# A hybrid encoder block: sums and low halves on GpSimd around each change of part of the down projection, its first pair reordered, and late query splits

## The chip, the cores and the metric

The kernel runs on one core of one Trainium2 chip. The metric is the device time of one execution in microseconds (us); what is compared are medians over several executions. A core has five engines that each work through their own queue in order: TensorE (PE, matrix products; its weight loads are listed apart as PEld), VectorE (DVE), ScalarE (ACT), GpSimd (POOL) and SyncE (SP), which here issues the transfers (DMA) between the device's memory and the on-chip buffer SBUF. PE writes its results to a second, small buffer, PSUM. Engines wait for each other through semaphores.

## The reference, cut to what matters

```python
h = x                                                     # 2048 x 1024, float32
xn = rms_norm(h, ln_mix_g)
proj = xn @ w_in
y_a = mlstm_group(...)                                    # 4 heads x 128, both directions
y_b = mla_group(...)                                      # 4 heads, softmax over 2048 keys
h = h + concatenate([y_a, y_b]) @ w_out
# conv_gated_mlp, D_FF = 2816
u = dwconv3_centred(rms_norm(h, ln_ffn_g) @ w_up, conv_w, conv_b)
gate, val = split(u, 2)
h = h + (silu(gate) * val) @ w_down
# per-layer input
gate = sigmoid(rms_norm(h, ple_norm_g) @ w_ple_gate)
h = h + gate * rms_norm(p @ w_ple_proj, ple_post_g)
out = rms_norm(h, final_g)
```

The change touches the attention and mLSTM stage (only when its steps are issued), the projection `w_down`, and the last stage.

## The kernel before, in words

**Precision.** All products are float32 results made of three products: each operand is split into a high half (a rounded copy, by ACT) and a low half (the operand less its high half, by DVE: a subtraction, line 120, in `split`), and `mm3` (line 130) adds low x high, high x low and high x high into PSUM. So one product of two 128-wide blocks is three PE instructions.

**Stages.** `run` issues them in order: the input projection, attention with the mLSTM as a side generator beside it, the output projection, `up_down` (up projection, convolution, down projection), and `ple` (the last stage, whose preparation runs as a generator beside the last pairs of down). All instructions are issued by one Python program; a scheduler then sets the order on each engine, so that the order of the built program can differ from the order of the lines. SBUF is divided into named places (`self.at("t7", ...)`); a second tile at the same place waits until the readers of the first are done. Places and PSUM tiles are what couples the steps.

**Attention** (from line 1000). 64 steps (head, query tile), each with a written order of operations; every "." in it is a place where `pump` may advance the mLSTM generator, `SIDE` of 832 times in all. In the generator, `pause(n)` yields n times between a step's vector work and its products. `load_q` and `split_q` load the queries of a pair of query tiles and split them.

**Up and down** (`up_down`, line 1387 on). Each stage is cut into *pairs* i: pairs 0 to 21 are the first half of the sequence of the up projection (block 0), 22 to 43 the second (block 1), and 44 to 51, 52 to 59 and 60 to 67 are down, whose inner dimension (22 tiles of 128) is cut into three parts of 8, 8 and 6 tiles (blocks 2 to 4); part after part is added to h. Within a pair the 2 x 2 blocks are multiplied with seven products in place of eight (Strassen's scheme in Winograd's form): A11 B11, S1 T1, S2 T2, A12 B21, S3 T3, A22 T4 and S4 B22, each of 12 PE instructions of 128x512 (9 in block 4). The right-hand tiles B and T belong to a block and stay in SBUF for all its pairs; at a *change of part* they are loaded and split anew, by `load_op`, tile by tile, through a few rotating raw buffers ("opr"). The left-hand tiles belong to a pair: `up_load` loads them two pairs ahead (in down: "hraw", the hidden activations that the convolution stored), `up_prep` makes the four sums S1 to S4 of them one pair ahead (four 128x512 additions, lines 1361 to 1369) and splits them by `up_pair` ("fw").

The seven products of a pair go to two PSUM tiles, one with halves x and y ("fxy"), one with halves z and spare ("fzs"). The products A22 T4 and S4 B22 of a pair are issued in the next pair (`rest(prev)`), where they add to y and z. In the up projection, results go to "ug" and "uv", which `conv` takes through the convolution and the gate to `hid_d`. In down they are added to two rows of h ("fh", loaded by `down_out` into five rotating places, o[0] and o[1], stored when the pair is done). p1, a copy of the first product, is made by ACT (line 1493) for i up to 44.

Pair 44 is special: it is down's first, and `conv` of pair 43 runs inside it; the second row of h is loaded to the place "u2", which is uv of pair 43, so its load (line 1325) is issued when that convolution is done. The adds of p1, T3 and z into that row follow the load.

**The last stage** (`ple`, the loop over 16 tiles of 128 rows). For each: the products with `w_ple_proj` ("pjp"), the next tile's p load (line 1580) and transposes ("nt_p", line 1603), the load of h for the tile after (line 1587) with its square sum ("junk", line 1589) and normalisation ("xn", line 1594), 48 products with `w_ple_gate` in two halves of columns, then the final norm: squares (line 1688), reduction (1692), gain (1690 and 1693), scale and two stores (1695 to 1698). h has three places in turn, so the load for tile st + 2 waits until the stores of tile st - 1 have gone out.

Of the kernel before, what the change touches and what calls it, by code (L numbers as in the profile page):

```python
# [19 lines left out]
P = 128  # L20
# [16 lines left out]
LAG_T, LAG_X, LAG_R = 1, 2, 2  # L37
SIDE = 621
KSCALE = 128.0 ** -0.5
# [21 lines left out]
class Block:  # L61
# [679 lines left out]
    def mlstm(self):  # L741
# [17 lines left out]
        def state(r, j, kk, v1, old, new):  # L759
            kn, kw = kk[:, 0], kk[:, 1]  # L760
            nc.vector.scalar_tensor_tensor(kw, kn, KSCALE, hc("w", r, j).unsqueeze(2).broadcast_to([P, NH, P]),
                                           op0=ALU.mult, op1=ALU.mult)
            yield from pause(6 if (r, j) == (1, 0) else 3)
            for hp in range(2):
# [35 lines left out]
        for c in range(NT):  # L800
# [21 lines left out]
            if c == 0:  # L822
                yield from pause(5)
            mk2 = self.at("w9", [P, 2, NH, P], name="mk")
# [135 lines left out]
    def attend(self, side):  # L960
# [60 lines left out]
        for i, (h, qt) in enumerate(seq):  # L1021
# [8 lines left out]
            nxt = start(*seq[i + 1]) if i + 1 < len(seq) else None  # L1030
            if qt % 2 == 0 and i + 2 < len(seq):
                split_q(seq[i + 2][0], seq[i + 2][1] // 2)
            if nxt is None:
                self.ps0 = self.pml.tile([P, 512], F32, name="wo0", tag="ml")
                self.out_mm(self.ps0, self.y0, range(4), slice(0, 512))
            for op in order:
# [6 lines left out]
                elif op == "X" and nxt:  # L1043
                    soft(nxt)
                elif op[0] == "e" and nxt:
                    expo(nxt, int(op[1]))
                elif op[0] == "E" and i:
                    expo(cur, int(op[1]))
                elif op == "V" and qt % 2:
                    pend = Tile()  # L1050
                    pend.h, pend.pr, pend.pts = h, qt // 2, pts
                    pv(pend, 0)
                elif op == "V" and pend is not None:
                    pv(pend, 1)
            if qt % 2:
                pts = []
# [201 lines left out]
    def load_op(self, blk, n):  # L1258

        ops = self.xop[n] = self.op_places(blk, n)  # L1260
        for k, (hi, lo) in enumerate(ops):
# [11 lines left out]
            self.nc.sync.dma_start(raw, src)  # L1273
            self.split(raw, hi, lo)

# [65 lines left out]
    def up_prep(self, i):  # L1341
# [15 lines left out]
        else:  # L1357
            sv, sg = flat(raw[1]), g
            lo, hi = slice(0, n // 2), slice(n // 2, n)
            tt = nc.vector.tensor_tensor  # L1360
            tt(sv[:, hi], sv[:, lo], sv[:, hi], op=ALU.add)
# [14 lines left out]
    def up_down(self, out):  # L1376
# [90 lines left out]
        for i in range(n):  # L1467
# [16 lines left out]
            x, s.y, s.z, s.spare = xy[:, 0], xy[:, 1], zs[:, 0], zs[:, 1]  # L1484
            prod(x, s.ops["A11"], "B11")
            if s.down:
                s.o = outs.pop(i)
                add(s.o[0][:, H], s.o[0][:, H], x)
            if i > NUP:
                add(twice(s.o[1]), twice(s.o[1]), x.unsqueeze(1).broadcast_to([P, 2, SB]))  # L1490
            else:
                s.p1 = self.at(f"t{6 + i % 2}", [P, SB], name="p1")
                nc.scalar.copy(s.p1, x)
            if i == 0:
# [39 lines left out]
            if i == NUP - 1:  # L1534
                outs[NUP] = self.down_out(NUP, (0,))
            if i == NUP:
                s.o += self.down_out(NUP, (1,))
                add(twice(s.o[1]), twice(s.o[1]), s.p1.unsqueeze(1).broadcast_to([P, 2, SB]))
            if s.down and i + 1 < n:
                outs[i + 1] = self.down_out(i + 1)  # L1540
            prod(s.y, s.ops["S3"], "T3", True)
            if s.down:
                add(s.o[1][:, H], s.o[1][:, H], s.y)
# [19 lines left out]
    def ple(self, out):  # L1563
# [99 lines left out]
        for st in range(NT):  # L1663
# [15 lines left out]
            for i in range(len(cuts) - 1):  # L1679
# [8 lines left out]
                nc.scalar.activation(gt[:, fs], h2[:, fs], AF.Square, accum_out=s2[:, i:i + 1])  # L1688
                if cuts[i + 1] < D:
                    nc.vector.tensor_tensor(h2[:, fs], h2[:, fs], gfin[:, fs], op=ALU.mult)  # L1690
            st2 = self.stat(1, "ps3")
            nc.vector.tensor_reduce(st2, s2, axis=AX.X, op=ALU.add)  # L1692
            nc.vector.tensor_tensor(h2[:, fs], h2[:, fs], gfin[:, fs], op=ALU.mult)
            r2 = self.rsq(st2, 1, 1.0 / D)
# [51 lines left out]
```

## Time and profile before

| | |
|---|---|
| median of 3 executions | 2996.68 us (2990.95 to 2999.37) |
| profiled execution, its own time | 2998.91 us |
| its span in the profile | 2997.1 us |
| granted PE clock, mean | 0.994 |
| PE busy / DVE / ACT / POOL | 98% / 69% / 45% / 5% of the span |
| PE busy, 1255 to 1800 us (up projection, first half, and what leads to it) | 542.11 of 545 us |
| PE busy, 1800 to 2300 us (up projection, second half, and the start of down) | 492.03 of 500 us |
| PE busy, 2300 to 2750 us (down) | 429.53 of 450 us |
| PE busy, 2750 to 2997 us (last stage) | 232.94 of 247 us |

How rows of the profile are read. A timeline row has its start and length in us, the engine, the line, the operation, the names (out<-in), shapes, the count of like instructions in a row, and in brackets the idle time before it with what ended it: `[10.88 <-DVE fh L1380]` means that the engine stood 10.88 us and was released by the DVE instruction of line 1380 that wrote fh. A wait row ("engine line waited for") has the total, the number of times and the longest. A group row has busy time and mean ns of one, then the idle time before. A row "SPq" is the issue of a transfer; the transfer itself lands some us later. A window row has start:end and length, then busy time and count for PE, PEld, DVE, ACT and POOL, the granted PE clock, the DMA engines' share and GB/s. A row of one line or operation gives shortest/median/longest duration in ns.

### The profile page before, as it was taken

How to read it: one execution, taken by the hardware profiler on the slowest of the kernel's cores; microseconds unless marked ns; L12 is line 12 of the kernel's file. 1: busy time of each engine (PE TensorE's matmuls, PEld its weight loads, DVE VectorE, ACT ScalarE, POOL GpSimd, SP SyncE). 2: the span in 40 equal slices, each digit the busy share in tenths (PEclk: the TensorE clock that was granted, in tenths of full speed). 3: DMA queues.
4: the chain of work that ended last, by engine and by line, in shares of the span. 5: the costliest groups of instructions: out<-in, count | busy, mean ns of one | idle time of the engine just before them, and what ended most of it. 6: DMA issues, size and time to landing. Idle time of an engine off the chain costs nothing. (4 is left out here: it accounts for less than half of the span.)

```text
span 2997.1 us, 40676 instructions
## 1 busy us (share of the span) xinstructions
PE 2926.3 (98%) x14858; PEld 2457.2 (82%) x14858; DVE 2069.6 (69%) x3798; ACT 1347.3 (45%) x2645; POOL 148.0 (5%) x262
## 2 busy tenths in 40 slices
PE   8999999999999999999999999999998999999998
PEld 7888888888898888888788887788886787877777
DVE  7431556667777677636888888877779778787555
ACT  7211545555666565523544445444445132233444
POOL 3100000000000001001000000000000000000111
PEclk9999999999999999999999999999999999999999
DMA  6522445343333333568664345833336868575221
GB/s 196 107 76 88 137 130 165 109 149 99 102 101 97 94 124 105 177 211 277 221 216 138 136 140 191 263 123 125 127 122 195 266 216 291 185 247 182 73 77 64
DMA packets 377400, 460.19 MB, mean 154 GB/s; under 512 B 30176, under 2 KB 263152, under 8 KB 377200
## 3 DMA queue, kind: packets, MB, share of 16 engines
q1 hardware_dynamic: 377200, 457.59, 47.5%
q8 instruction: 117, 1.92, 0.3%
q14 instruction: 83, 0.68, 0.1%
HBM read 294.26 MB, written 163.25 MB: 153 GB/s over the span
## 5 line engine op out<-in xcount | busy, mean ns | idle before, releaser
L130 PE MATMUL fxy<-op,fw 128*128 128x512 f32 x3168 | 754.1, 395 | 15.9 <-DVE fh L1380 8.4
L130 PEld LDWEIGHTS fxy<-op,fw 128*128 128x128 f32 x3168 | 591.4, 189 | 162.1 <-DVE fh L1380 19.2
L130 PE MATMUL fzs<-op,fw 128*128 128x512 f32 x1584 | 385.8, 389 | 0.8 <-DVE xt L1151 0.8
L130 PEld LDWEIGHTS fzs<-op,fw 128*128 128x128 f32 x1584 | 297.1, 188 | 63.0 <-DVE xt L1151 1.0
L130 PE MATMUL bk<-wsp,xh 128*128 128x512 f32 (+1 forms) x768 | 234.4, 386 | 1.1 <-DVE wsp L126 1.1
L117 ACT CAST pt<-tb 128x512 fp32r<-128x512 f32 x256 | 146.5, 587 | 194.5 <-PE tb L976 193.9
L918 DVE TENSOR_REDUCE mx<-bk 128x1 f32<-128x512 f32 x256 | 174.8, 685 | 46.3 <-PE bk L917 45.4
L130 PE MATMUL fxy<-op,fwd 128*128 128x512 f32 x792 | 193.1, 393 | 12.8 <-DVE fh L1380 10.9
L130 PE MATMUL ppv<-pt,kv 128*128 128x256 f32 x1536 | 203.0, 287 | 0.0
L120 DVE TENSOR_TENSOR pt<-tb,pt 128x512 fp32r<-128x512 f32 x256 | 174.0, 686 | 33.6 <-ACT pt L117 31.9
L130 PEld LDWEIGHTS ppv<-pt,kv 128*128 128x128 f32 x1536 | 188.7, 191 | 0.4 <-ACT pt L117 0.4
L130 PEld LDWEIGHTS fxy<-op,fwd 128*128 128x128 f32 x792 | 149.3, 189 | 46.0 <-DVE fh L1380 12.1
L936 ACT ACTIVATE pe<-bk,nm 128x512 f32<-128x512 f32 x256 | 174.5, 696 | 25.4 <-DVE nm L930 24.5
L130 PE MATMUL pgp<-pw,x3s 128*128 128x512 f32 (+1 forms) x792 | 179.0, 385 | 0.8 <-DVE pw L120 0.8
L130 PE MATMUL bk<-wo,yhl 128*128 128x512 f32 x744 | 175.6, 392 | 0.0
L130 PEld LDWEIGHTS pgp<-pw,x3s 128*128 128x128 f32 x792 | 144.4, 188 | 29.7 <-DVE pw L120 1.1
L130 PEld LDWEIGHTS bk<-wsp,xh 128*128 128x128 f32 x768 | 144.6, 189 | 27.5 <-DVE wsp L126 2.4
L130 PEld LDWEIGHTS bk<-wo,yhl 128*128 128x128 f32 x744 | 138.2, 188 | 28.0
L1380 DVE TENSOR_TENSOR fh<-fh,fxy 128x512 f32<-128x512 f32 x143 | 108.4, 770 | 75.8 <-PE fxy L130 74.6
L130 PE MATMUL bk<-wsp,xl 128*128 128x512 f32 (+1 forms) x384 | 150.7, 392 | 7.4 <-DVE xl L120 7.4
L130 PE MATMUL bk<-xh,wqk 128*128 128x512 f32 x480 | 157.3, 393 | 0.0
L117 ACT CAST fw<-hraw 128x1024 fp32r<-128x1024 f32 (+1 forms) x72 | 70.5, 981 | 187.3 <-PE fxy L130 114.6
(327 smaller groups left out, 5030.0 us busy)
## 6 DMA issues: line engine op xcount, KB each, us to landing
fwr<-in_w_up SPq DMA_DIRECT2D x66, 512.0 KB, 4.2
fh<-h_d SPq DMA_DIRECT2D x48, 512.0 KB, 4.8
h_d<-fh SPq DMA_DIRECT2D x48, 512.0 KB, 2.9
s_d<-fwr SPq DMA_DIRECT2D x44, 512.0 KB, 3.2
fws<-s_d SPq DMA_DIRECT2D x44, 512.0 KB, 3.7
rw<-row_d SPq DMA_DIRECT2D x32, 512.0 KB, 5.2
hraw<-hid_d SPq DMA_DIRECT2D x30, 512.0 KB, 4.8
tsum<-in_w_down SPq DMA_DIRECT2D x44, 256.0 KB, 4.4
```

Of the source, the lines that this page charges most:

```text
L117: nc.scalar.copy(hi, src)
L120: (sub or nc.vector).tensor_tensor(lo, src, _f(hi), op=ALU.subtract)
L130: mm = lambda *a, **k: self.nc.tensor.matmul(*a, **k, skip_group_check=more)
L918: nc.vector.tensor_reduce(s.mx[:, kb:kb + 1], ps, axis=AX.X, op=ALU.max)
L936: nc.scalar.activation(s.pe[:, kb % 2], s.banks[kb], AF.Exp, bias=s.nm, scale=ASCALE, accum_out=s.rs[:, kb:kb + 1])
L1380: add = lambda o, a, b: tt(o, a, b, op=ALU.add)
```

## The change

In words, by the parts of the diff:

- The mLSTM generator is advanced 629 times rather than 621 over the attention, and two of its pauses are four yields longer.
- `split_q` is called behind a step's order of operations instead of ahead of it.
- `load_op`: the low halves of T4 and B22 of the three down blocks are subtracted on GpSimd.
- `up_prep`: for the pairs 44 to 46, 51 to 54 and 59 to 62 the four sums are made on GpSimd.
- `up_down`: pair 45 copies its first product as well (to the spare half of its second PSUM tile, where pairs 0 to 44 use an SBUF place), and the adds of pairs 44 and 45 read the copy. In pair 44 the sum p1 + T3 + z is made in "t7"; only then the second row of h is loaded, and p1 and that sum are added to its two halves. The rows of pair 45 are loaded behind that, not ahead of T3.
- `ple`: for all but the last tile the second half's gain is multiplied ahead of the reduction rather than behind it.

```diff
--- before.py
+++ after.py
@@ -35,7 +35,7 @@
 EPS = 1e-6
 SB = 512
 LAG_T, LAG_X, LAG_R = 1, 2, 2
-SIDE = 621
+SIDE = 629
 KSCALE = 128.0 ** -0.5
 ASCALE = 192.0 ** -0.5
 
@@ -760,7 +760,7 @@
             kn, kw = kk[:, 0], kk[:, 1]
             nc.vector.scalar_tensor_tensor(kw, kn, KSCALE, hc("w", r, j).unsqueeze(2).broadcast_to([P, NH, P]),
                                            op0=ALU.mult, op1=ALU.mult)
-            yield from pause(6 if (r, j) == (1, 0) else 3)
+            yield from pause(10 if (r, j) == (1, 0) else 3)
             for hp in range(2):
                 ps = mbank([P, 2, 256])
                 for i in range(2):
@@ -820,7 +820,7 @@
                 else:
                     nc.sync.dma_start(kk[:, 0], self.kn_d[c])
             if c == 0:
-                yield from pause(5)
+                yield from pause(9)
             mk2 = self.at("w9", [P, 2, NH, P], name="mk")
             qi2 = self.at("w10", [P, 2, NH, P], name="qi")
             for r in range(2):
@@ -1028,8 +1028,6 @@
             if qt % 2 == 1 and i + 3 < len(seq):
                 load_q(seq[i + 3][0], seq[i + 3][1] // 2)
             nxt = start(*seq[i + 1]) if i + 1 < len(seq) else None
-            if qt % 2 == 0 and i + 2 < len(seq):
-                split_q(seq[i + 2][0], seq[i + 2][1] // 2)
             if nxt is None:
                 self.ps0 = self.pml.tile([P, 512], F32, name="wo0", tag="ml")
                 self.out_mm(self.ps0, self.y0, range(4), slice(0, 512))
@@ -1052,6 +1050,8 @@
                     pv(pend, 0)
                 elif op == "V" and pend is not None:
                     pv(pend, 1)
+            if qt % 2 == 0 and i + 2 < len(seq):
+                split_q(seq[i + 2][0], seq[i + 2][1] // 2)
             if qt % 2:
                 pts = []
             cur = nxt
@@ -1257,6 +1257,7 @@
 
     def load_op(self, blk, n):
 
+        nc = self.nc
         ops = self.xop[n] = self.op_places(blk, n)
         for k, (hi, lo) in enumerate(ops):
             raw = self.at(next(self.orot), [P, SB], name="opr")
@@ -1271,7 +1272,7 @@
             else:
                 src = self.w_down(blk - 2, k, 2 * (int(n[1]) - 1) + int(n[2]) - 1)
             self.nc.sync.dma_start(raw, src)
-            self.split(raw, hi, lo)
+            self.split(raw, hi, lo, sub=nc.gpsimd if blk > 1 and n in ("T4", "B22") else None)
 
     def up_load(self, i):
 
@@ -1357,7 +1358,8 @@
         else:
             sv, sg = flat(raw[1]), g
             lo, hi = slice(0, n // 2), slice(n // 2, n)
-            tt = nc.vector.tensor_tensor
+            change = any(-2 < i - bl[0] < 3 for bl in self.BLOCKS[2:])
+            tt = (nc.gpsimd if change else nc.vector).tensor_tensor
             tt(sv[:, hi], sv[:, lo], sv[:, hi], op=ALU.add)
             tt(sv[:, lo], g[:, lo], sv[:, lo], op=ALU.subtract)
         ops["S3"], ops["S1"] = self.up_pair(sv)
@@ -1483,14 +1485,15 @@
             xy, zs = self.two([P, 2, SB], "fxy"), self.two([P, 2, SB], "fzs")
             x, s.y, s.z, s.spare = xy[:, 0], xy[:, 1], zs[:, 0], zs[:, 1]
             prod(x, s.ops["A11"], "B11")
+            if i < NUP + 2:
+                s.p1 = s.spare if i > NUP else self.at(f"t{6 + i % 2}", [P, SB], name="p1")
+                nc.scalar.copy(s.p1, x)
             if s.down:
                 s.o = outs.pop(i)
-                add(s.o[0][:, H], s.o[0][:, H], x)
+                p1 = s.p1 if i < NUP + 2 else x
+                add(s.o[0][:, H], s.o[0][:, H], p1)
             if i > NUP:
-                add(twice(s.o[1]), twice(s.o[1]), x.unsqueeze(1).broadcast_to([P, 2, SB]))
-            else:
-                s.p1 = self.at(f"t{6 + i % 2}", [P, SB], name="p1")
-                nc.scalar.copy(s.p1, x)
+                add(twice(s.o[1]), twice(s.o[1]), p1.unsqueeze(1).broadcast_to([P, 2, SB]))
             if i == 0:
                 load(0, "B21")
             load(then, "B11")
@@ -1533,13 +1536,18 @@
                 conv(prev)
             if i == NUP - 1:
                 outs[NUP] = self.down_out(NUP, (0,))
-            if i == NUP:
-                s.o += self.down_out(NUP, (1,))
-                add(twice(s.o[1]), twice(s.o[1]), s.p1.unsqueeze(1).broadcast_to([P, 2, SB]))
-            if s.down and i + 1 < n:
+            if i > NUP and i + 1 < n:
                 outs[i + 1] = self.down_out(i + 1)
             prod(s.y, s.ops["S3"], "T3", True)
-            if s.down:
+            if i == NUP:
+                c22 = self.at("t7", [P, SB], name="c22")
+                add(c22, s.p1, s.y)
+                add(c22, c22, s.z)
+                s.o += self.down_out(NUP, (1,))
+                add(s.o[1][:, L], s.o[1][:, L], s.p1)
+                add(s.o[1][:, H], s.o[1][:, H], c22)
+                outs[i + 1] = self.down_out(i + 1)
+            elif s.down:
                 add(s.o[1][:, H], s.o[1][:, H], s.y)
                 add(s.o[1][:, H], s.o[1][:, H], s.z)
             else:
@@ -1686,11 +1694,12 @@
                 nc.vector.tensor_tensor(pj[:, fs], pj[:, fs], gt[:, fs], op=ALU.mult)
                 nc.vector.tensor_tensor(h2[:, fs], h2[:, fs], pj[:, fs], op=ALU.add)
                 nc.scalar.activation(gt[:, fs], h2[:, fs], AF.Square, accum_out=s2[:, i:i + 1])
-                if cuts[i + 1] < D:
+                if st < NT - 1 or cuts[i + 1] < D:
                     nc.vector.tensor_tensor(h2[:, fs], h2[:, fs], gfin[:, fs], op=ALU.mult)
             st2 = self.stat(1, "ps3")
             nc.vector.tensor_reduce(st2, s2, axis=AX.X, op=ALU.add)
-            nc.vector.tensor_tensor(h2[:, fs], h2[:, fs], gfin[:, fs], op=ALU.mult)
+            if st == NT - 1:
+                nc.vector.tensor_tensor(h2[:, fs], h2[:, fs], gfin[:, fs], op=ALU.mult)
             r2 = self.rsq(st2, 1, 1.0 / D)
             nc.vector.tensor_scalar(h2[:, 0:512], h2[:, 0:512], r2, None, op0=ALU.mult)
             nc.sync.dma_start(out[0, st * P:(st + 1) * P, 0:512], h2[:, 0:512])
```

## The prediction, made blind

> **What bounds the kernel now.** I read the busy shares first, then what TensorE (PE) waited for, then stretches of 150 us through the down projection, then the order of single instructions where a stretch falls short.
>
> ```profile
> span 2997.1 us, 40676 instructions
> PE 2926.3 (98%) x14858; PEld 2457.2 (82%) x14858; DVE 2069.6 (69%) x3798; ACT 1347.3 (45%) x2645; POOL 148.0 (5%) x262
> ...
> PE fxy L130 <- DVE fh L1380: 19.3, 8, 10.9
> PE nt_p L1603 <- DVE xn L1594: 6.1, 9, 1.0
> PE mb L768 <- DVE kk L761: 2.8, 1, 2.8
> ...
> 2100.00:2250.00 150.00, 150.00 (x662) 123.58 (x661) 108.54 (x127) 67.00 (x87) 0.00 (x0) 1.00 0.39 125
> 2250.00:2400.00 150.00, 130.24 (x542) 104.03 (x541) 120.74 (x166) 52.18 (x73) 0.00 (x0) 0.94 0.72 232
> 2400.00:2550.00 150.00, 147.08 (x636) 119.29 (x635) 116.70 (x161) 44.25 (x58) 0.00 (x0) 0.99 0.74 252
> ```
>
> PE is busy for 2926.3 of 2997.1 us, so only its idle time, 70.8 us, and time at a lowered clock can be won without taking products out, and the change takes none out. In the stretch columns (span, then PE, PEld, DVE, ACT, POOL busy with their counts, granted clock, DMA share, GB/s) the stretch from 2100 shows PE full: 662 products in 150 us, 0.2266 us each. From 2250, where the up projection turns into down, there are 120 fewer: 120 x 0.2266 = 27.2 us lost, of them 150 - 130.24 = 19.8 idle and 7.4 at a clock of 0.94. From 2400 (change to the second part of down) 26 fewer lose 5.9, of them 2.9 idle. Those two places are what the change can mostly reach. The next view shows them, product by product.
>
> ```profile
> 2295.74 3.02 PE L130 MATMUL fxy<-op,fw 128*128 128x512 f32 x12 [2.02 <-ACT p L1493]
> 2299.63 3.02 PE L130 MATMUL fxy<-op,fw 128*128 128x512 f32 x12 [0.88 <-DVE fh L1380]
> 2304.44 7.36 PE L130 MATMUL fxy<-op,fw 128*128 128x512 f32 x24 [1.79 <-DVE fw L120]
> 2311.63 2.88 PE L130 MATMUL fzs<-op,fw 128*128 128x512 f32 x12
> 2325.40 4.68 PE L130 MATMUL fxy<-op,fwd 128*128 128x512 f32 x12 [10.88 <-DVE fh L1380]
> ...
> 2478.88 10.03 PE L130 MATMUL fxy<-op,fw 128*128 128x512 f32 x36 [2.92 <-DVE fh L1380]
> ```
>
> These rows are, by the order of the built program: T2 of pair 44, its B21, then its T3 between two halves of B11 of pair 45, T1 of 45, and T4 of 44, which waits 10.88 us. The 12 products behind the wait take 4.68 instead of 2.88. At 2478.88 stands the same thing, smaller, in pair 52.
>
> Who is late at 2325.40? VectorE (DVE) and the SP queue say it:
>
> ```profile
> 2289.01 3.10 DVE L120 TENSOR_TENSOR op<-opr,op 128x512 fp32r<-128x512 f32 x5
> ...
> 2306.11 1.28 DVE L1423 SCALAR_TENSOR_TENSOR fgv<-ug,fcw,fgv 128x1024 f32<-128x1024 f32 x1
> 2314.86 1.22 DVE L120 TENSOR_TENSOR fw<-hraw,fw 128x1024 fp32r<-128x1024 f32 x1
> 2318.67 0.68 DVE L1380 TENSOR_TENSOR fh<-fh,fxy 128x512 f32<-128x512 f32 x1
> 2322.92 1.23 DVE L1380 TENSOR_TENSOR fh<-fh,p 128x1024 f32<-128x1024 f32 x1 [1.39 <-DMA fh<-h_d]
> 2324.66 0.68 DVE L1380 TENSOR_TENSOR fh<-fh,fxy 128x512 f32<-128x512 f32 x1
> ...
> 2317.30 0.33 SPq L1325 DMA_DIRECT2D fh<-h_d  x1
> ```
>
> Two things in a row. DVE works through a queue (splits, convolution of pair 43, sums of the next pair's tiles) and comes to the add of B21 only at 2318.67, though those products, begun at 2299.63, had ended before 2304.44. Then the load of h, issued at 2317.30 because its buffer holds the last convolution, is waited for until 2322.92, and T3's add comes at 2324.66. T4 writes the PSUM buffer which that add reads.
>
> **The change part by part.**
>
> *First pair of down.* Its correction term c22 = p1 + T3 + z is added up in an SBUF buffer before h is there, so PSUM is free without the load. Leaving the load and its 1.23 us add out alone brings the two adds of T3 and z from 2324.66 to about 2319.3 (right behind 2318.67 + 0.68): -5.4 us. p1 is copied by ScalarE for pairs 44 and 45 at once; the row at 2295.74 shows what such a copy can cost, 2.02 us, and in the new order it stands ahead of the copies of streamed tiles that wait for DMAs, so I take up to that off. What moves behind: the add of h's load for pair 45 now also waits for loads queued later on SP, and T1 of pair 45 waits for it. Product order in the built program: T2(44), B21(44) and T3(44) with B11(45) in three pieces between them, T2(45), T4(44), B22(44), B21(45), T1(45). By T4 there are 60 products in either order, and T1(45) comes 31 products x 0.2266 = 7.0 us behind T4's start at the earliest, where a load (5.6 us from 2317.30 to 2322.92) fits. I cost it at nothing; without that cover it is 1 to 3 us.
>
> *Work taken from DVE.* Low halves of T4 and B22 (8 per change of part, 6 in the last) and four sums for each of 11 pairs (three or four to a change), 66 operations of 128x512 in all, go to GpSimd (POOL). Five splits in a row take 3.10 (0.62 each), so until T4(44) DVE gives up 8 splits and 4 to 8 sums, 7 to 10 us of its 25 us queue. POOL takes them up. Before's trace has no two-input POOL operation of that size:
>
> ```profile
> L140 POOL TENSOR_TENSOR rsr<-rsm,nhalf 128x1 f32<-128x1 f32 (+2 forms) x96 | 67.3, 702 | 8.0
> L830 POOL TENSOR_SCALAR_AFFINE_SELECT mk<-rw 128x512 f32<-128x512 f32 x32 | 25.7, 827 | 912.0 <-PE mb L768 547.5 <-PE mb L853 273.9 <-DVE mx L918 68.6
> ...
> 910.62 1.67 POOL L830 TENSOR_SCALAR_AFFINE_SELECT mk<-rw 128x512 f32<-128x512 f32 x2 [23.59 <-DVE mx L918]
> ...
> 910.88 0.92 DVE L835 TENSOR_TENSOR qi<-qk,rw 128x512 f32<-128x512 f32 x1
> 911.79 1.04 DVE L835 TENSOR_TENSOR qi<-qk,rw 128x512 f32<-128x512 f32 x1
> ...
> L830 POOL TENSOR_SCALAR_AFFINE_SELECT mk<-rw x32: 634/638/1169, 663.0 to 1197.9; 128x512 f32<-128x512 f32 x32
> ...
> L835 DVE TENSOR_TENSOR qi<-qk,rw x32: 665/914/1046, 659.4 to 1199.2; 128x512 f32<-128x512 f32 x32
> ```
>
> Bounds: 0.70 us (a POOL tensor-tensor of one column, nearly all fixed cost) and 1.65 (two selects of 0.827 mean, one per input). I take 1.2, the middle, as nothing puts it nearer to either. [...]
>
> ```profile
> 2301.30 1.21 ACT L117 CAST op<-opr 128x512 fp32r<-128x512 f32 x2 [0.26 <-DMA opr<-in_w_down]
> 2308.02 1.05 ACT L117 CAST fw<-hraw 128x1024 fp32r<-128x1024 f32 x1 [5.51 <-DVE hraw L1362]
> ```
>
> The queue on POOL by the program: T4's four subtractions, three sums of pair 45, then B22's with the last sum. The last streamed raw tile lands at 2301.3, so with some seven operations then still ahead the fourth sum ends near 2301 + 7 x 1.2 = 2309.4; a copy by ScalarE and a split by DVE (1.05 and 1.22) make the S2 weights ready at 2311.7, against 2316.1 before (2314.86 + 1.22). T2(45) waits for them. Behind that split on DVE stand, by the program, what is left of the convolution (two or three operations of 1.28 like the row at 2306.11), the short ones for its edge, and c22, which so comes near 2317, 5 us later. PE: 48 products from T2(44)'s start without the 2.02, at 2293.7, end at 2304.6 plus 1 or 2 us of small waits; it then waits some 5 us for T2(45), and some 3 for c22. T4(44) starts at 2317 rather than 2325.4: -8.4. The lost clock I leave as it is (two shorter waits for one long one); at best 4 us of its 7.4 come back. Range of this part: -13 to +6 (the rival below).
>
> *Second part of down.* The wait of 2.92 stands behind an add of DVE that is queued among eight splits of streamed tiles (0.62 each), each waiting for its load's copy. These go to POOL. The wait and its slow clock (36 products in 10.03 rather than 36 x 0.2266 = 8.2) are worth 2.9 + 1.8 = 4.7; I take -2.9, bounds -4.7 and +3. The third part shows no wait worth naming and is put at 0.
>
> *The last loop (per-layer input).* For 15 tiles the second gain multiply stands ahead of the reduce, and the built program has the next p load ahead of both output stores on SP.
>
> ```profile
> 2861.61 0.33 SPq L1696 DMA_DIRECT2D out<-h  x1
> 2862.04 0.55 SPq L1580 DMA_DIRECT2D p_t<-in_p_turned  x1
> 2862.64 0.60 SPq L1698 DMA_DIRECT2D out<-h  x1
> 2865.39 0.33 SPq L1587 DMA_DIRECT2D h<-h_d  x1
> ...
> 2868.97 1.06 ACT L1589 ACTIVATE junk<-h 128x1024 bf16<-128x1024 f32 x1 [3.62 <-DMA h<-h_d]
> ...
> 2859.64 0.15 DVE L1692 TENSOR_REDUCE ps<-ps 128x1 f32<-128x2 f32 x1 [0.85 <-ACT gate L1688]
> 2859.71 0.68 DVE L1693 TENSOR_TENSOR h<-h,gpf 128x512 f32<-128x512 f32 x1
> ...
> 2871.96 1.23 PE L1603 MATMUL nt_p<-ident,xn 128*128 128x128 f32 x8 [0.67 <-DVE xn L1594]
> ```
>
> The loop's round is a chain: second output store, load of h into the freed buffer, square, normalisation, transposes. Without p's issue (0.55) between the stores the round shortens by up to 0.55, the wait of 0.67 almost wholly. Against that the reduce moves behind the multiply: DVE was idle 0.85 ahead of the reduce, waiting for the square, so the multiply (0.68) may fit there, and if it doesn't, it costs 0.68. Nine waits cost 6.1; I take half, -3. Bounds: -6.1, and +6 (9 x 0.68).
>
> *Pauses and late query splits.* The side generator's count (629 for 621) and two longer pauses move mLSTM work against attention. In the built program the product that waits 2.76 for kk keeps its place in PE's queue, and the query splits still come some two tiles ahead of their use: 0, bounds ±2.8.
>
> Sum: -8.4 - 2.9 - 3 + 0 = -14.3. The profiled execution took 2998.91 us (1.8 around its span), 2.2 above the median of 2996.68, so 2984.6; I don't take the 2.2 off again, as single runs lay from 2990.95 to 2999.37, and say 2984.
>
> **The rivals.**
>
> *DVE and POOL hold each other up.* In the rows at 910 two selects and two DVE multiplies with SBUF inputs took 2.2 us together, where alone they take 2 x 0.634 and 2 x 0.665 (the fastest of each), 2.6 in series: beside each other they hardly run faster than one after the other. If each POOL operation stops DVE for its whole length, 20 of them up to the end of pair 45 cost 20 x (1.2 - 0.62) = 11.6 us of DVE's queue. From T4(44) that takes back the 5.4 of the load and 6 more: +6. In the second part the 20 cost as much, less DVE's idle share there (116.70 of 150 busy, so 22% of some 36 us, 8): +4. With -3 in the last loop: +7, 3006. It decides from a POOL operation of 0.62 + 5.4/20 = 0.9 us on. For it: the slowed multiplies, and a saturated DVE. Against it: adds that read PSUM have one SBUF input, and a select of 0.83 beside a multiply of 0.92 isn't a full stop. [...]
>
> *The wait only moves.* POOL at its upper bound, 1.65, ends the fourth sum at 2312.6; S2 is ready at 2314.9, c22 at 2320.5, and T1(45) then waits 2 us for a load behind the convolution's store. Gain -5 + 2 = -3 there, 0 in the second part, -3 at the end: 2993. For it: ACT, DVE and POOL serve these steps in order. Against it: loads land in 3 to 5 us.
>
> *The last loop lengthens.* The multiply doesn't fit into the 0.85 and the store gains nothing: +6 in place of -3, 2993.6.
>
> *It does not do what it says:* late query splits and longer pauses, whose order in the program scarcely moves; this is in the sum already at 0.
>
> **How the numbers follow.** Forecast 0.55, hold-up 0.20, moved wait 0.20, longer last loop 0.05. A measurement here tells 0.3%, about 9 us, from no change: faster is below 2987.7, slower above 3005.7. Of the forecast's 0.55, 0.50 is faster and 0.05 same (its own range 2972 to 2990); the moved wait gives 0.05 faster and 0.15 same; the hold-up 0.05 same and 0.15 slower; the last loop 0.03 faster and 0.02 same. Faster 0.58, same 0.27, slower 0.15. Low end: -13 - 4.7 - 6.1 = -24, with the spread of runs 2968 (some 0.05 below); high end 3004, which leaves out most of the hold-up.
>
> **What would show it.** T4 of pair 44 no longer waits 10.9 us for an fh add, and what it waits for is c22 or a POOL subtraction; T2(45) waits for fw by some 5 us. From 2250 PE gets 575 to 600 products in 150 us, not 542. POOL rows of 128x512 near 1.2 us; DVE's 128x512 splits stay near 0.69 beside them (if they rise to 1 or more, the hold-up is true). The 2.92 at pair 52 is gone. Waits of nt_p fall to 3 us. The forecast is wrong if POOL needs over 2 us for an operation, if DVE rows stretch, or if new waits for fw or hraw in pairs 45, 46, 53 and 61 take back more than 8 us.

## The result, and the profile after

The changed kernel takes 3007.07 us (median of 5, 3005.11 to 3008.71) beside 2993.4 us (5 runs, 2990.95 to 2999.37) of the kernel before: a ratio of 1.0042, 95% interval 1.0027 to 1.0056. It is slower by 8 to 17 us where 12.7 less were forecast (2984 from 2996.68). The profiled execution is the one of 3007.07 us.

The first rows are from the page of the changed kernel (busy times) and from PE's waits in it (total, times, longest):

```profile
span 3005.1 us, 40700 instructions
PE 2927.8 (97%) x14858; PEld 2462.4 (82%) x14858; DVE 2048.3 (68%) x3733; ACT 1350.5 (45%) x2646; POOL 239.3 (8%) x328
...
PE fxy L130 <- DVE fh L1382: 21.1, 12, 5.5
PE fxy L130 <- ACT fzs L1490: 9.1, 1, 9.1
```

GpSimd has 66 instructions and 91.3 us more, VectorE only 21.3 us less: an operation that VectorE did in some 0.62 us takes GpSimd about 1.4, and of the some 40 us of work (66 x 0.62) that were moved off VectorE only about half are gone from its busy time. The wait of 10.9 us is gone from the list, one of 9.1 for ScalarE is new, and those for fh are twelve rather than eight. The transposes' waits in the last stage (nt_p, 6.1 us before) don't appear any more. The stretches through the down projection (columns as before) show the place of the loss:

```profile
2250.00:2400.00 150.00, 134.19 (x556) 107.29 (x555) 115.00 (x146) 53.72 (x77) 31.84 (x20) 0.94 0.70 228
2400.00:2550.00 150.00, 140.19 (x598) 112.40 (x597) 102.31 (x131) 43.07 (x57) 35.94 (x24) 0.98 0.71 242
2550.00:2700.00 150.00, 143.13 (x612) 114.55 (x611) 102.74 (x139) 42.57 (x61) 30.02 (x22) 0.99 0.61 210
```

The third of them in the kernel before:

```profile
2550.00:2700.00 150.00, 149.36 (x650) 120.44 (x649) 117.50 (x175) 45.29 (x65) 0.00 (x0) 1.00 0.65 217
```

At the first change 556 products instead of 542: 14 x 0.2266 = 3.2 us won. At the second 598 instead of 636, 8.6 us lost; at the third, where before 650 stood in the stretch and nothing worth naming was waited for, 612, another 8.6 lost. The second and third change hold no reordered pair; all that is new there is GpSimd's work. Such counts are of one execution each and differ by themselves: two kernels below that take the same time, down_ple and late_split, have 570 and 594 products in the first of these stretches, at granted clocks of 0.94 and 0.98.

The order of single instructions around the first change (PE, then ScalarE, GpSimd and VectorE; the last row of PE and of VectorE is from the second change) shows what T2 of pair 45 now waits for:

```profile
2327.00 5.49 PE L130 MATMUL fxy<-op,fw 128*128 128x512 f32 x12 [9.13 <-ACT fzs L1490]
2332.29 3.10 PE L130 MATMUL fxy<-op,fwd 128*128 128x512 f32 x12
2488.68 9.11 PE L130 MATMUL fxy<-op,fw 128*128 128x512 f32 x29 [5.53 <-DVE fh L1382]
...
2322.21 1.05 ACT L117 CAST fw<-hraw 128x1024 fp32r<-128x1024 f32 x1 [6.19 <-POOL hraw L1371]
2326.37 0.57 ACT L1490 COPY fzs<-fxy 128x512 f32<-128x512 f32 x1
...
2304.65 6.68 POOL L120 TENSOR_TENSOR op<-opr,op 128x512 fp32r<-128x512 f32 x4 [19.31 <-DMA opr<-tw_d]
2311.28 2.28 POOL L1363 TENSOR_TENSOR hraw<-hraw 128x512 f32<-128x512 f32 x1
2316.28 4.68 POOL L120 TENSOR_TENSOR op<-opr,op 128x512 fp32r<-128x512 f32 x3
2320.92 1.26 POOL L1371 TENSOR_TENSOR hraw<-hraw 128x512 f32<-128x512 f32 x1
...
2305.56 1.18 DVE L120 TENSOR_TENSOR fwd<-hraw,fwd 128x512 fp32r<-128x512 f32 x1
2308.41 4.01 DVE L1425 SCALAR_TENSOR_TENSOR fgv<-ug,fcw,fgv 128x1024 f32<-128x1024 f32 x2
2313.19 0.69 DVE L1382 TENSOR_TENSOR fh<-fh,fxy 128x512 f32<-128x512 f32 x1 [0.78 <-PE fxy L130]
2323.29 1.23 DVE L120 TENSOR_TENSOR fw<-hraw,fw 128x1024 fp32r<-128x1024 f32 x1 [5.89 <-ACT fw L117]
2330.08 0.69 DVE L1382 TENSOR_TENSOR c<-c,fzs 128x512 f32<-128x512 f32 x1
2486.80 1.22 DVE L120 TENSOR_TENSOR fw<-hraw,fw 128x1024 fp32r<-128x1024 f32 x1 [5.37 <-ACT fw L117]
```

Read from the bottom of the chain: GpSimd's fourth sum of pair 45 stands behind three subtractions of streamed tiles and ends at 2322.18. ScalarE's copy of that sum had been waiting 6.19 us for it. VectorE's split of the same sum, the last thing that T2's weights need, is done at 2324.52. Behind the copy of the sum in ScalarE's queue, and behind four steps of the convolution and one more copy, stood the copy of p1 of pair 45 (fzs from fxy), done at 2326.94. T2 of pair 45 writes the other half of the PSUM tile that this copy reads, and it starts at 2327.00. So of its 9.13 us some 6.7 would have been waited for the weights in any case, and the copy adds the rest. T4 of pair 44 then follows without a wait of its own, at 2332.29; c22, which it also needs, was done at 2330.77, as it stood in VectorE's queue behind that split. Both ways lead back to GpSimd's fourth sum.

And VectorE is slowed while GpSimd works: two operations of the convolution, at 2308.41, take 4.01 us instead of about 2.5 (1.28 each at 2325.47 and 2326.79, with GpSimd idle), a split of 128x512 takes 1.18 (at 2305.56) instead of 0.68 (at 2336.63, with GpSimd idle), while the add that reads PSUM keeps its 0.69 (at 2313.19).

### The profile page after: what moved, and what is told of

It reads as the page before. It is cut to its first block, busy times and chain, and to the rows that moved or that the text cites. A ratio compares the mean times of both kernels' runs of the same rounds, so it can differ in the third digit from the quotient of the medians.

```text
span 3005.1 us, 40700 instructions
## 1 busy us (share of the span) xinstructions
PE 2927.8 (97%) x14858; PEld 2462.4 (82%) x14858; DVE 2048.3 (68%) x3733; ACT 1350.5 (45%) x2646; POOL 239.3 (8%) x328
## 5 line engine op out<-in xcount | busy, mean ns | idle before, releaser
L1382 DVE TENSOR_TENSOR fh<-fh,fxy 128x512 f32<-128x512 f32 (+1 forms) x139 | 105.0, 767 | 84.8 <-PE fxy L130 84.2
```

The costliest lines, as they stand in the source:

```text
L1382: add = lambda o, a, b: tt(o, a, b, op=ALU.add)
```

## The experiments

Each ratio is against the kernel before, run beside it on the same chip; differences in us below are differences of ratios times 2997. By the intervals, a difference between two of these kernels is uncertain by 5 to 6 us either way.

| kernel | what it has | median us | before | ratio, 95% interval |
|---|---|---|---|---|
| changed kernel | all parts | 3007.07 | 2993.4 | 1.0042 [1.0027, 1.0056] |
| no_pool | without GpSimd's new work | 2979.53 | 2996.92 | 0.9943 [0.9930, 0.9955] |
| no_sums | low halves on GpSimd | 2989.36 | 2996.92 | 0.9975 [0.9964, 0.9986] |
| no_low | sums on GpSimd | 3003.53 | 2996.92 | 1.0025 [1.0015, 1.0036] |
| only_ple | before + gain ahead of the reduction | 2986.91 | 2996.92 | 0.9968 [0.9956, 0.9981] |
| only_down | before + first pairs reordered | 2988.75 | 2996.49 | 0.9973 [0.9962, 0.9984] |
| only_att | before + pauses, count, late splits | 3000.43 | 2996.49 | 1.0010 [1.0001, 1.0018] |
| sums34 | no_pool + sums of 8 pairs on GpSimd | 3001.42 | 2996.49 | 1.0017 [1.0008, 1.0027] |
| beside | no_pool + unused two-input work on GpSimd | 3011.14 | 2996.49 | 1.0042 [1.0028, 1.0056] |
| down_ple | before + first pairs + gain | 2979.53 | 2997.04 | 0.9936 [0.9922, 0.9950] |
| late_split | down_ple + late splits | 2979.16 | 2997.04 | 0.9939 [0.9927, 0.9951] |
| beside_one | as beside, one input | 2988.02 | 2997.04 | 0.9971 [0.9958, 0.9984] |
| beside_none | as beside, writes only | 2982.54 | 2997.04 | 0.9948 [0.9931, 0.9964] |

### no_pool: the changed kernel without work on GpSimd

```diff
-            self.split(raw, hi, lo, sub=nc.gpsimd if blk > 1 and n in ("T4", "B22") else None)
+            self.split(raw, hi, lo)
...
-            tt = (nc.gpsimd if change else nc.vector).tensor_tensor
+            tt = nc.vector.tensor_tensor
```

> The changed kernel with the sums and the low halves back on VectorE. Theory (the work on GpSimd is what costs: each 128x512 operation takes 1.3 to 2.2 us there, and ScalarE and VectorE, which work in order, stand behind it): the second and third part of down get back the 38 products each that they lost in 150 us, 2 x 8.6 = 17 us, so about 2990, and less if the first pair's reordering then pays; 2978 to 2990. Rival 1 (the reordering of the first pair is the loss, since T2 of pair 45 now waits for a ScalarE copy): the 9.1 us wait stays, 3000 or more. Rival 2 (the longer pauses and later query splits are the loss): 3000 or more as well, with attention's waits as in the changed kernel.

2979.53 us, 29.7 us less than the changed kernel by the ratios (0.0099 x 2997; 24 to 35). The same three stretches of this kernel:

```profile
2250.00:2400.00 150.00, 138.82 (x588) 111.90 (x587) 123.56 (x171) 55.02 (x77) 0.00 (x0) 0.97 0.74 243
2400.00:2550.00 150.00, 148.09 (x642) 120.63 (x641) 120.53 (x166) 44.78 (x59) 0.00 (x0) 0.99 0.75 252
2550.00:2700.00 150.00, 150.00 (x655) 121.22 (x654) 118.07 (x176) 44.87 (x65) 0.00 (x0) 1.00 0.65 220
```

32, 44 and 43 products more than in the changed kernel: 119 x 0.2266 = 27 of the 29.7 us. Both rivals fall: the reordered pairs and the attention edits are in this kernel, and it beats the one before by 13 to 21 us. In the first stretch the comparison holds one thing more: here, as in only_down below, T4 of pair 44 stands ahead of T2 of pair 45 in PE's queue, in the changed kernel behind it.

### no_sums and no_low: one kind of work on GpSimd each

no_sums has only the second of no_pool's two edits (the sums are back on VectorE), no_low only the first.

> The changed kernel with only the sums S1 to S4 back on VectorE; the low halves of T4 and B22 stay on GpSimd. If the sums are the loss (four in a chain, 5.2 us at best instead of 2.5, with copies and splits queued behind): near the kernel without any GpSimd work, within 4 us. If the low halves are the loss: near 3005.

> The changed kernel with only the low halves back on VectorE; the sums stay on GpSimd. If the sums are the loss: 2998 to 3007, with ScalarE's copies of hraw still waiting for GpSimd. If the low halves are the loss: 2978 to 2990.

A single culprit was expected. no_low lies where it was put for the sums as the loss, but no_sums is not within 4 us of no_pool: the 22 low halves alone cost 9.6 us (0.9975 against 0.9943), the 44 sums alone 24.6 (1.0025), both together 29.7. The sums are the larger share, and the low halves are not free.

### sums34 and beside: waiting for GpSimd, or slowed by it

sums34 puts the sums on GpSimd for the pairs 51 to 54 and 59 to 62 alone. In beside, VectorE does all of that itself, as in no_pool, and GpSimd makes four additions per pair at the same places, which nobody reads:

```diff
+            if change:
+                z = self.at("t7", [P, SB], name="beside")
+                m = n // 2
+                for _ in range(4):
+                    nc.gpsimd.tensor_tensor(z[:, :m], _f(d[:, 0]), _f(d[:, 1]), op=ALU.add)
             tt(sv[:, hi], sv[:, lo], sv[:, hi], op=ALU.add)
```

> The changed kernel without low halves on GpSimd, and with the sums there only for the changes to the second and third part (8 of the 11 pairs). Theory (products wait for the sums, through the queues of ScalarE and VectorE): each of the two stretches of 150 us loses 40 products as in the changed kernel, 8 to 9 us each, so 15 to 18 us above the 2979.5 without GpSimd work: 2994 to 2998. If only the first change is the loss: under 2984.

> The changed kernel with all sums and low halves on VectorE, and for the same 8 pairs four additions of the same size on GpSimd whose result nobody reads. It separates waiting for GpSimd from being slowed by it. If the engines hold each other up (the hold-up of the prediction): most of what the sums on GpSimd cost, 10 us and more above 2979.5, with VectorE's rows stretched. If it is the waiting for results: under 4 us above 2979.5.

sums34 is 22.2 us above no_pool (0.0074), 4 more than the theory of waiting gave, which is within the uncertainty; the two later changes are thus the larger part of the 24.6 us of all sums. beside, in which nothing waits for GpSimd, is 29.7 us above no_pool (0.0099): 32 operations, 0.93 us each. So the hold-up exists and alone can cost as much as the whole change; waiting for results isn't needed for it. The groups of one stretch, 2430 to 2520, by line, operation and shape (busy, mean ns), first of no_pool:

```profile
L120 DVE TENSOR_TENSOR op<-opr,op 128x512 fp32r<-128x512 f32 x28 | 17.9, 686 | 2.8 <-ACT op L117 2.8
L1382 DVE TENSOR_TENSOR fh<-fh,fxy 128x512 f32<-128x512 f32 x23 | 15.5, 682 | 9.4 <-PE fxy L130 9.4
L1364 DVE TENSOR_TENSOR hraw<-hraw 128x512 f32<-128x512 f32 x4 | 2.7, 686 | 0.0
```

and of beside (the lines are five further on):

```profile
L120 DVE TENSOR_TENSOR op<-opr,op 128x512 fp32r<-128x512 f32 x28 | 21.5, 812 | 0.0
L1387 DVE TENSOR_TENSOR fh<-fh,fxy 128x512 f32<-128x512 f32 x18 | 12.2, 680 | 10.8 <-PE fxy L130 10.8
L1369 DVE TENSOR_TENSOR hraw<-hraw 128x512 f32<-128x512 f32 x4 | 6.3, 1565 | 0.1
L1376 DVE TENSOR_TENSOR hraw<-hraw 128x512 f32<-128x512 f32 x4 | 3.8, 951 | 0.0
L1367 POOL TENSOR_TENSOR beside<-fwd 128x512 f32<-128x512 f32 x16 | 26.3, 1641 | 1043.0 <-DVE fwd L120 1042.0
```

VectorE's second sum takes 1565 ns instead of 686, its fourth 951; adds with one input from PSUM stay at 680. Who waits for that is PE: its waits for fh adds, in no_pool 12.3 us (6 of them), are in beside

```profile
PE fxy L130 <- DVE fh L1387: 33.3, 15, 4.6
```

The order of single instructions at the first four of these additions shows what happens:

```profile
2433.50 1.67 DVE L1369 TENSOR_TENSOR hraw<-hraw 128x512 f32<-128x512 f32 x1
2435.09 0.67 DVE L1387 TENSOR_TENSOR fh<-fh,fzs 128x512 f32<-128x512 f32 x1
2435.68 1.18 DVE L1375 TENSOR_TENSOR hraw<-hraw 128x512 f32<-128x512 f32 x1
2436.79 2.31 DVE L120 TENSOR_TENSOR fw<-hraw,fw 128x1024 fp32r<-128x1024 f32 x1
2439.02 1.75 DVE L1376 TENSOR_TENSOR hraw<-hraw 128x512 f32<-128x512 f32 x1
...
2432.82 7.40 POOL L1367 TENSOR_TENSOR beside<-fwd 128x512 f32<-128x512 f32 x4 [991.31 <-DVE fwd L120]
```

By themselves VectorE's three sums and its split take 3 x 0.69 + 1.22 = 3.3 us, and four additions on GpSimd 4 x 1.26 = 5.0 (1.26 by the rows of the changed kernel below). One after the other that is 8.3, and from 2432.82 to 2440.77 they took 7.95. So here the two engines nearly take turns; only the add that reads PSUM, at 2435.09, keeps its 0.67.

The price in the changed kernel's own stretch lies on GpSimd's side as well. Durations there (shortest, median, longest ns) of two of its operations:

```profile
L120 POOL TENSOR_TENSOR op<-opr,op x22: 1257/1424/2278, 2304.7 to 2653.2; 128x512 fp32r<-128x512 f32 x22
L1371 POOL TENSOR_TENSOR hraw<-hraw x11: 1257/1611/2159, 2283.2 to 2665.6; 128x512 f32<-128x512 f32 x8, 128x384 f32<-128x384 f32 x3
```

1.26 us undisturbed (the sum at 2320.92, with VectorE idle), up to 2.28 where VectorE has two inputs from SBUF too (the sum at 2311.28, beside the two operations of the convolution). In the changed kernel VectorE is relieved of the moved work but its queue waits for results: PE's two longest waits in down, 9.13 and 5.53 us, both come behind a split for which VectorE had idled, 5.89 and 5.37 us, until ScalarE had copied a sum of GpSimd. In beside it keeps the work and waits for nothing. So the changed kernel pays by waiting as well, and GpSimd's own slowing lengthens that waiting. How its 29.7 us divide between waiting and slowing is not separated, as no run has the waiting alone.

### beside_one and beside_none: what of GpSimd's work holds VectorE up

The additions of beside are replaced by eight multiplications by 1.0 with one input from SBUF, or by one addition of a single column and ten constant fills:

```diff
-                for _ in range(4):
-                    nc.gpsimd.tensor_tensor(z[:, :m], _f(d[:, 0]), _f(d[:, 1]), op=ALU.add)
+                for _ in range(8):
+                    nc.gpsimd.tensor_scalar(z[:, :m], _f(d[:, 0]), 1.0, None, op0=ALU.mult)
```

```diff
+                nc.gpsimd.tensor_tensor(z[:, 0:1], _f(d[:, 0, 0:1]), _f(d[:, 1, 0:1]), op=ALU.add)
+                for _ in range(10):
+                    nc.gpsimd.memset(z[:, :m], 0.0)
```

> As the kernel with unused additions on GpSimd beside all work on VectorE, but in their place eight operations with a single input from SBUF. If what slows VectorE is GpSimd's reading of SBUF of any kind: VectorE's 128x512 additions of two SBUF inputs stay stretched (1 us and more, from 0.69), and 10 us or more above 2979.5. If it takes two inputs on both sides: rows of 0.69 and under 5 us.

> The same with one short anchor and ten GpSimd operations that only write SBUF (constant fill, 128x512). If reading is what holds VectorE up: its rows stay at 0.69 and the time within 4 us of 2979.5. If any use of SBUF by GpSimd does: rows stretched, and 5 us or more above.

Eight one-input operations per pair cost 8.4 us (0.9971 against 0.9943; 3 to 14), though GpSimd is busy there about twice as long as in beside; ten fills cost 1.5, within the intervals of nothing. Groups of the same stretch, of beside_one and then of beside_none:

```profile
L1369 DVE TENSOR_TENSOR hraw<-hraw 128x512 f32<-128x512 f32 x4 | 3.1, 788 | 0.0
L1376 DVE TENSOR_TENSOR hraw<-hraw 128x512 f32<-128x512 f32 x5 | 4.9, 984 | 0.1
L1387 DVE TENSOR_TENSOR fh<-fh,fxy 128x512 f32<-128x512 f32 x22 | 14.8, 679 | 8.1 <-PE fxy L130 8.1
L1367 POOL TENSOR_SCALAR beside<-fwd 128x512 f32<-128x512 f32 x31 | 51.7, 1668 | 23.9 <-ACT fwd L117 21.6
```

```profile
L1370 DVE TENSOR_TENSOR hraw<-hraw 128x512 f32<-128x512 f32 x4 | 2.8, 688 | 0.0
L1368 POOL MEMSET beside<- 128x512 f32 x39 | 20.6, 528 | 2.2
```

Fills leave VectorE's sums at 688 ns with GpSimd busy for 20.6 us of the stretch; one input stretches them to 788 to 984; two to 951 to 1565. So neither form of the expectation for beside_one holds as put, by its rows: here GpSimd operations that read SBUF hold VectorE up and fills do not, and two inputs do so far more than one (29.7 us for 32 operations, 8.4 for 64). It also shows that beside's cost isn't that of having more instructions or of another buffer kept alive, since in these two GpSimd reads the same tile, if only a column of it in beside_none, and writes to the same place.

### only_down, only_ple, only_att: the other parts alone

Each is the kernel before with one part of the change's diff.

> The kernel before with only the reordering of the first pairs of down (copy of p1, c22 ahead of the load of h). Theory: the stretch from 2250 to 2400 gets about the 588 products it has without GpSimd work, 46 more than before, 46 x 0.2266 = 10.4 us; so 6 to 11 us less than before. Rival: the wait only moves to T2 or T1 of pair 45, and under 4 us come back.

> The kernel before with only the gain multiplied ahead of the reduction in the last stage. Theory: the nine waits of the transposes (6.1 us) go, as they did in the changed kernel, and so 4 to 7 us less than before. Rival: those waits went because earlier stages ended in another order, and this alone changes less than 2 us.

> The kernel before with only the longer pauses, the count of 629 and the late query splits. By the prediction 0, within 2.8 us either way. From the waits of the runs so far (products waiting for ACT pe: 6.3 to 7.6 us where these edits are in, 4.7 to 5.0 where not) rather 1 to 3 us more than before.

only_down gains 8.1 us (0.9973; 5 to 11 by the interval). Its stretch from 2250:

```profile
2250.00:2400.00 150.00, 137.25 (x571) 110.78 (x570) 121.88 (x170) 54.37 (x76) 0.00 (x0) 0.94 0.72 239
```

The time is as expected (6 to 11), the stretch is not: 571 products, 29 more than before (6.6 us), not 46. Its products around T4 of pair 44, and one add on VectorE:

```profile
2299.38 11.30 PE L130 MATMUL fxy<-op,fw 128*128 128x512 f32 x36 [4.73 <-DVE fh L1382]
2311.75 2.99 PE L130 MATMUL fxy<-op,fwd 128*128 128x512 f32 x12 [1.07 <-DVE c L1382]
...
2325.03 4.79 PE L130 MATMUL fxy<-op,fw 128*128 128x512 f32 x11 [4.86 <-DVE fh L1382]
...
2323.09 0.69 DVE L1382 TENSOR_TENSOR fh<-fh,p 128x512 f32<-128x512 f32 x1 [2.39 <-DMA fh<-h_d]
```

T4 waits 1.07 us for c22 instead of 10.88 for the load. Two waits for adds, 4.73 and 4.86, take the rest of what was there to gain. The first is as long as the three of 2.02, 0.88 and 1.79 that stood there before, together. The second is new: the add that ends it stands in VectorE's queue behind the one at 2323.09, which waits for the moved load of h.

only_ple gains 9.6 us (5.7 to 13.2), where 4 to 7 were expected. Transposes of one tile in the kernel before, then those of two tiles and the issues on SP in only_ple:

```profile
2856.34 1.23 PE L1603 MATMUL nt_p<-ident,xn 128*128 128x128 f32 x8 [0.82 <-DVE xn L1594]
```

```profile
2849.40 1.03 PE L1605 MATMUL nt_p<-ident,xn 128*128 128x128 f32 x8
...
2863.97 1.03 PE L1605 MATMUL nt_p<-ident,xn 128*128 128x128 f32 x8
...
2865.48 0.55 SPq L1582 DMA_DIRECT2D p_t<-in_p_turned  x1
2866.71 0.33 SPq L1699 DMA_DIRECT2D out<-h  x1
2867.09 0.42 SPq L1701 DMA_DIRECT2D out<-h  x1
```

p's load is ahead of both stores, and a round takes 2863.97 - 2849.40 = 14.57 us, with PE never waiting; before it took 2871.96 - 2856.34 = 15.62.

only_att costs 3.0 us, its interval just above nothing (0.3 to 5.4).

### down_ple and late_split: what pays, put together

down_ple is no_pool with the attention as before; late_split adds the late query splits to it.

> The kernel before with the two parts that paid alone: the reordered first pairs of down and the gain ahead of the reduction, nothing on GpSimd, attention as before. If the parts add up: before less 8 less 10, and about 4 below the 17 to 18 us that the same kernel with the attention edits gained, so 2975 to 2979 beside a before of 2996.5. If the attention edits cost only through what follows them: as that kernel, near 2979.

> down_ple with only the query splits behind the order of operations (pauses and count as before). If the late splits are what costs in attention: 3 to 5 us above down_ple. If the pauses are: within 2 us of down_ple.

0.9936 and 0.9939, against 0.9943 of no_pool, which has all the attention edits: three intervals that overlap almost wholly. down_ple gains 19.2 us, its two parts alone 8.1 and 9.6. What the attention edits cost is at most a few us. The late splits are not seen to cost anything (0.9 us). The traces point to the longer pauses and the count: the first product of the up projection starts at 1435.7 to 1441.6 us (mean 1439.0) in the nine kernels with all attention edits, and at 1431.4 to 1437.5 (mean 1434.9) in the five without the pauses, late_split's at 1434.3. That is one execution of each, so it is not settled. All three beat the kernel before, by 17 to 19 us, and the changed kernel by about 30.

## Why the prediction was wrong, by its own steps

**What bounds the kernel** was right in the main: nearly all that the runs gain and lose lies in the stretches from 2250 and in the last loop.

**First pair of down: right about the load, and close in size partly by luck.** Forecast 5.4 for the load plus up to 2.0 for the copy, measured 8.1 alone (5 to 11). T4's wait for the load went. But the copy's 2.0 did not come back (one wait of 4.73 for 2.02, 0.88 and 1.79), and the wait behind the moved load, put at nothing, or 1 to 3 us without cover, is 4.86. In the changed kernel little of the gain is left (3.2 us in its stretch, where 8.4 were forecast), because of the next step.

**Work taken from DVE: this is the step that failed.** It set 1.2 us for a GpSimd operation, took it as running beside VectorE, and counted VectorE's relief as a gain. The 0.70 of its lower bound is a mean of three forms: of the 96 operations of line 140 those of one column took 0.61 us, of two 0.73, of four 1.04. That nearly all of it is fixed cost was the author's estimate. The moved operation takes 1.26 us when nothing disturbs it, so the middle of the bounds was near; but beside VectorE's two-input work it takes up to 2.28, and VectorE's sums of two SBUF inputs take 0.3 to 0.9 us longer beside such work (beside). Measured cost of moving the work: 29.7 us. In the first place the prediction had seven operations left on GpSimd from 2301, at 1.2 us, and the fourth sum ready at 2309.4. The trace has eleven from 2304.65, at 1.6 us each, and the fourth sum at 2322.18. So c22 came at 2330.77 rather than near 2317. T2 of pair 45 did wait as this part said, but 9.1 us rather than 5: first for the split weights, then for the copy of p1. The prediction had put that copy "ahead of the copies of streamed tiles"; it stood behind a copy waiting for GpSimd.

**Second part of down: wrong in sign**, -2.9 forecast, +8.6 in the stretch. The wait of 2.92 us did not go: it stands in the same run of 48 products of pair 52, at 2488.68 (19 and 29 products there, 12 and 36 before), and is 5.53 us long. With all of that work on VectorE (no_pool) it is 1.91. **Third part: 0 forecast, +8.6.** The step looked for waits to remove and found none; 22 operations are moved to GpSimd there, and their cost on a stretch that was full of products wasn't counted.

**The last loop: right in direction, off in size.** -3 forecast, with -6.1 as the bound; measured -9.6, its interval 5.7 to 13.2. The bound came from the wait rows alone. But a round fell from 15.62 us to 14.57, 1.05 us for each of the nine waiting tiles, 9.5 in all: beside the wait of 0.67 the transposes behind it took 1.23 rather than 1.03, and some 0.2 more stands in no row.

**Attention: 0 forecast, with 2.8 either way; +3.0 measured alone** (0.3 to 5.4), nothing measurable between down_ple, late_split and no_pool. Zero lies just outside that interval, so the pauses may cost a little more than the step said.

The parts add up within their uncertainty: -8.1 - 9.6 + 3.0 = -14.7, beside -17.1 for no_pool, which has these three. With the 29.7, which is itself the changed kernel less no_pool, that is +15.0 beside +12.6 (8 to 17) for the change.

**The rival that came true** is the hold-up of VectorE and GpSimd, given 0.20 and 3006 us. Its deciding point was 0.9 us for an operation, and the undisturbed 1.26 is above it. It came true in its mechanism: where both engines have two inputs from SBUF they nearly take turns (7.95 of 8.3 us at the first additions of beside). Its total is close by luck: its terms were +6, +4 and -3 in the first, second and last place, and nothing in the third and in attention, where the runs show -3.2, +8.6, -9.6, +8.6 and +3.0. The row that the prediction set against it (a select of 0.83 beside a multiply of 0.92 is no full stop) was of a GpSimd operation with one input; beside_one shows that such rows say little of two inputs (VectorE's sums at 788 to 984 ns there, 951 to 1565 in beside).

## What to carry to other kernels

Moving two-input elementwise work from VectorE to GpSimd need not be a gain where VectorE itself reads two SBUF operands: here about half of the relief was lost again, and each such GpSimd operation that nobody even waited for (in beside) cost 0.93 us of the end. Before counting such a move as a gain, compare like forms in the trace (inputs from SBUF on both sides), and price it at every place to which it applies, the full ones too. A copy or split that waits for a slower engine also holds up what is queued behind it on its own engine (here ScalarE's copy of the fourth sum waited 6.19 us, and the copy of p1 stood behind it), and a PSUM tile shared by two halves can pass that on to products that write the other half (here some 2.4 of T2's 9.13 us).

## What the runs showed of the hardware

VectorE's 128x512 sums of two SBUF inputs go from 0.69 us (no_pool) to 0.95 to 1.57 (means by line, 2430 to 2520) beside a GpSimd addition with two SBUF inputs (beside), to 0.79 to 0.98 beside a multiplication with one (beside_one), and stay at 0.69 beside constant fills (beside_none); VectorE's adds with one PSUM input stay at 0.68 in all of them. In beside the two engines nearly take turns: 7.95 us for work that is 8.3 one after the other. One-input work costs 8.4 us for 64 operations, two-input work 29.7 for 32. Through what the engines hold each other up, and why one input costs so much less than two, is not shown.

Waits cost a second time, as the products behind a long one ran at a lower granted clock: in the changed kernel the 12 products behind the wait of 9.13 us took 5.49 instead of 2.88, at 0.50 (2327.00 to 2332.49), and in the kernel before the 12 behind the wait of 10.88 took 4.68, at 0.62 (2325.40 to 2330.08; 1.00 in the 2.9 us that follow). In only_down the 11 behind a wait of 4.86 took 4.79, while the 12 behind one of 1.07 took 2.99 (0.94 over the 150 us that hold both).
